# The last norm of a hybrid decoder layer, by two parts of its tokens

## The chip, the cores and the metric

The kernel runs on one core of a Trainium2 chip. The metric is the device time of one launch in microseconds (us); times told of the whole kernel are medians of several runs. A profile is of one execution, and its own time stands beside its span below.

## The reference

One inference step of a one-layer decoder trunk, for a prompt of 256 tokens and 8 samples of 8 tokens, together 320 tokens of width 2048. The layer has two halves; the change lies in the end of the second:

```python
f, new_ffn_conv = conv_ffn(rms_norm(x, p["norm_ffn_pre"]), ffn_conv_state, ...)
x = x + rms_norm(f, p["norm_ffn_post"])

def rms_norm(x, w):
    y = x * lax.rsqrt(jnp.mean(x * x, axis=-1, keepdims=True) + EPS)
    return y * w

def conv_ffn(h, conv_state, w_up, conv_w, conv_b, w_down):
    up = h @ w_up
    up, new_conv = causal_depthwise_conv(up, conv_state, conv_w, conv_b)
    g, u = jnp.split(up, 2, axis=-1)
    return (jax.nn.gelu(g, approximate=True) * u) @ w_down, new_conv
```

The inner width is 5632. The norm at the end needs, for each token, the mean square over all 2048 outputs of the last product, so it can begin for a token only when every block of outputs of that token is there. The output y is x after this line; call x before it x1.

## The kernel before, in words

**Layout.** Features lie on the 128 partitions, tokens along the free axis: an activation of width 2048 is 16 blocks of 128 partitions x 320 tokens. Every product keeps the weights as the stationary operand (128 x 128) and streams the 320 tokens.

**Products.** Each f32 operand is split into two fp32r parts, hi and lo, and a product is three: hi x hi, hi x lo, lo x hi (`accumulate`, lines 127 to 131: line 129 weight hi with x hi, 130 weight hi with x lo, 131 weight lo with x hi). Each of the three loads its weights. `slab` (110 to 125) brings 128 x 1024 weights: a 512 KB DMA on SyncE's queue (115) into `wraw`, hi by a cast on ScalarE (118), lo by a subtraction on VectorE (120). All three tiles have 3 buffers.

**The feed-forward half.** The 5632 inner columns are taken in 11 chunks of 512. `ffn_up` (1061) makes a chunk's inner activations `fhi` and `flo`, 4 blocks of 128 x 320; it reads `h_hi` and `h_lo`, the split input of 16 blocks each. `chunk_out` (205) multiplies the chunk into the 16 output blocks: for each block 4 k-steps of three products into one PSUM bank (the pool `mm` has 4 banks, the pool `ms` 4 more), then VectorE adds the bank to `acc_ffn` in SBUF (217). One `slab` covers a pair of output blocks. The loop (1145 to 1152) makes chunk g + 1's activations before it multiplies chunk g out, so nothing but `chunk_out` is left for the last chunk.

**The last chunk.** Behind each block, `last` (1139) squares the block (ScalarE, lines 281 and 300) and adds the square to the sum `sq4`: on GpSimd (282) for blocks 1 to 12, on VectorE (302) for 13 and 14; block 15's square stays apart (`one`). Then ScalarE scales the block by the norm's weight (1142).

**The tail.** `token_sums` (258) adds over the partitions by products with a column of ones, for `sq4` and then for block 15's square; a product with f32 operands is two instructions in the trace. `rsqrt_by_root` (243) makes 1/sqrt from them, in six small operations on VectorE and one on ScalarE; `spread` (267) transposes the result so that it lies on all partitions, twice: one bank (`r4`) for VectorE, a second one that ScalarE copies to SBUF (`r4s`, 273) for GpSimd. Meanwhile `hand_over` (1159) multiplies blocks of x1 with the identity on TensorE, so that VectorE reads them from PSUM (`x1p`). VectorE makes y for blocks 0 to 10, two at a time (1186 the product with r, 1188 the addition of x1), GpSimd blocks 11 to 15 (1193, 1194); SyncE's queue sends VectorE's blocks (1189), ScalarE's queue GpSimd's (1195).

**Order.** The program is written against a scheduler which orders each engine's instructions by priority and by estimated readiness, gives out buffers and sets all semaphores. `tc.high_priority` (as `first()`) pulls instructions ahead; `tc.issue_after(x)` keeps instructions behind x. Each engine runs its own list in order.

Of the kernel before, what the change touches and what calls it, by code (L numbers as in the profile page):

```python
# [9 lines left out]
F32 = mybir.dt.float32  # L10
# [24 lines left out]
def hybrid_step(  # L35
# [68 lines left out]
    def first():  # L104

        return tc.high_priority(offset=200000)

    slab_load = []

    def slab(src, begins=False):  # L110
        n = src.shape[2]
        with tc.high_priority(offset=100000):
            m = n * src.shape[1]
            raw = wp.tile([P, 1024], F32, tag="wraw", name="wraw", bufs=3)
            slab_load.append(sp.dma_start(raw[:, :m].rearrange("p (a n) -> p a n", n=n), src).ins)
            hi = wp.tile([P, 1024], F32R, tag="whi", name="whi", bufs=3)
            for o in (slice(0, P), slice(P, m)) if begins else (slice(0, m),):
                act.copy(hi[:, o], raw[:, o])  # L118
            lo = wp.tile([P, 1024], F32R, tag="wlo", name="wlo", bufs=3)
            dve.tensor_tensor(out=lo[:, :m], in0=raw[:, :m], in1=hi[:, :m].bitcast(F32), op=ALU.subtract)  # L120

        def block(k, c):
            o = k * n + c * P
            return hi[:, o:o + P], lo[:, o:o + P]
        return block

    def accumulate(ps, w, xhi, xlo, first, last):
        whi, wlo = w
        pe.matmul(ps, whi, xhi, start=first, stop=False)  # L129
        pe.matmul(ps, whi, xlo, start=False, stop=False)  # L130
        return pe.matmul(ps, wlo, xhi, start=False, stop=last).ins  # L131
# [70 lines left out]
    acc = None  # L202
    pd_last = []

    def chunk_out(w, ck, hi, lo, begins, done=None, rate=1):

        for nb in range(KD):
            if nb % 2 == 0:
                wb = slab(rows_of(w, 4 * ck, 4, P * nb, 256))
            ps = mm.tile([P, 512], F32, tag="mm", name=f"pd_{ck}_{nb}")  # L210
            for k in range(4):
                made = accumulate(ps[:, :NT], wb(k, nb % 2), hi[:, k, :], lo[:, k, :], k == 0, k == 3)
            with first():
                if begins:
                    act.copy(acc[:, nb, :], ps[:, :NT])
                else:
                    dve.tensor_tensor(out=acc[:, nb, :], in0=acc[:, nb, :], in1=ps[:, :NT], op=ALU.add)  # L217
# [20 lines left out]
        rsqrt_ins.append(ins)  # L238
        return r

    rsqrt_ins, sums_ins = [], []

    def rsqrt_by_root(rest, ps, scale, rows=P):

        v = tp.tile([P, 3], F32, tag="rs_v3", name="rs_v")[:rows]
        r = tp.tile([P, 3], F32, tag="rs_r3", name="rs_r", bufs=3)[:rows]
        t = tp.tile([P, 3], F32, tag="rs_t3", name="rs_t")[:rows]
        s = tp.tile([P, 3], F32, tag="rs_s3", name="rs_s")[:rows]
        dve.tensor_scalar(out=v, in0=rest, scalar1=scale, scalar2=EPS, op0=ALU.mult, op1=ALU.add)
        dve.scalar_tensor_tensor(out=v, in0=ps, scalar=scale, in1=v, op0=ALU.mult, op1=ALU.add)  # L250
        act.activation(s, v, AF.Sqrt)
# [6 lines left out]
    def token_sums(*sqs):  # L258

        ps = misc("tsum")  # L260
        for c, o in enumerate((0, P, NT - P)):
            for i, sq in enumerate(sqs):
                ins = pe.matmul(ps[:, c:c + 1], sq[:, o:o + P], ones[:, 0:1], start=i == 0, stop=i == len(sqs) - 1).ins  # L263
        sums_ins.append(ins)
        return ps[:, 0:3]

    def spread(r, out=None):

        ps = misc("spread")
        for c, o in ((2, NT - P), (0, 0), (1, P)):  # L270
            pe.transpose(ps[:, o:o + P], r[:, c:c + 1].to_broadcast([P, P]), ident)
        if out is not None:
            act.copy(out, ps[:, :NT])
        return ps[:, :NT]

    def add_square(total, x, begins, adder=pool, place=("sq", 2)):
        if begins:
            act.activation(total, x, AF.Square)
        else:
            sq = tp.tile([P, NT], F32, tag=place[0], name="sq", bufs=place[1])  # L280
            act.activation(sq, x, AF.Square)
            adder.tensor_tensor(out=total, in0=total, in1=sq, op=ALU.add)

    def squares_of(total):

        one, held = [], []

        def step(nb):
            if nb < KD - 3:
                add_square(total, acc[:, nb, :], nb == 0)  # L290
                if nb == 0:

                    act.activation(tp.tile([P, 1], F32, name="root_there", bufs=1), total[:, 0:1], AF.Sqrt)
                return
            with first():
                if nb < KD - 1:
                    held.append(misc("sq_ps")[:, :NT])
                else:
                    one.append(tp.tile([P, NT], F32, tag="sq", name="sq", bufs=2))
                act.activation((one or held)[-1], acc[:, nb, :], AF.Square)  # L300
                if nb > KD - 3:
                    dve.tensor_tensor(out=total, in0=total, in1=held.pop(0), op=ALU.add)
        return step, one


    dacs_d = dr.tile([NH, NT + NS], F32, name="dacs_d")
# [748 lines left out]
    with tc.tile_pool(name="fp", bufs=1) as fp:  # L1055
# [80 lines left out]

        squares, one = squares_of(sq4)

        def last(nb):
            a = acc[:, nb, :]  # L1140
            squares(nb)
            act.activation(a, a, AF.Copy, scale=col(prm_at["norm"][2] + nb))

        NG = NF // 4
# [12 lines left out]
        x1p = {}  # L1157

        def hand_over(where, *blocks):
            for nb in blocks:  # L1160
                x1p[nb] = where[0].tile([P, 512], F32, tag=where[1], name="x1p")[:, :NT]
                made = pe.matmul(x1p[nb], ident, x1[:, nb, :], start=True, stop=True)
            return made.ins
        banks, more = (mm, "mm"), (ms, "ms")
        with tc.issue_after(pd_last[-1]):
            most = token_sums(sq4)
        with tc.issue_after(sums_ins[-1]):
            made = hand_over(banks, 0)
        with tc.issue_after(made):
            ps = token_sums(*one)  # L1170
        r = rsqrt_by_root(most, ps, 1.0 / D)
        with tc.issue_after(sums_ins[-1]):
            made = hand_over(banks, 1, 2)
        with tc.issue_after(made):
            r4 = spread(r)
            r4s = fp.tile([P, NT], F32, name="r4s")
            spread(r, r4s)
        hand_over(banks, 3)
        hand_over(more, 4, 5)
        hand_over(banks, 6, 7, 8, 9, 10)  # L1180
        made = None
        for ks in [slice(k, k + 2) for k in range(0, 10, 2)] + [slice(10, 11)]:
            f = acc[:, ks, :]
            n = ks.stop - ks.start
            with tc.issue_after(made) if made else nullcontext():
                dve.tensor_tensor(out=f, in0=f, in1=r4.unsqueeze(1).to_broadcast([P, n, NT]), op=ALU.mult)
            for k in range(n):
                made = dve.tensor_tensor(out=f[:, k, :], in0=f[:, k, :], in1=x1p[ks.start + k], op=ALU.add).ins
            sp.dma_start(o_y[:, ks, :], f)
        for ks in (slice(11, 12), slice(12, 14), slice(14, 16)):  # L1190
            f = acc[:, ks, :]
            n = ks.stop - ks.start
            pool.tensor_tensor(out=f, in0=f, in1=r4s.unsqueeze(1).to_broadcast([P, n, NT]), op=ALU.mult)
            pool.tensor_tensor(out=f, in0=f, in1=x1[:, ks, :], op=ALU.add)
            act.dma_start(o_y[:, ks, :], f)


_OUTS = [
# [81 lines left out]
```

## Time and profile before

| what | us |
|---|---|
| median of 3 runs | 1798.79 (1796.71 to 1799.12) |
| the profiled execution's own time | 1800.87 |
| its span, first to last instruction | 1799.2 |
| TensorE busy | 1776.3 (99%) |
| VectorE, ScalarE, GpSimd busy | 1190.1, 795.4, 295.4 |

A profile row gives an operation's line, engine, operands and shapes. PE is TensorE's products, PEld its weight loads, which overlap them; DVE is VectorE, ACT ScalarE, POOL GpSimd, SP SyncE. In a timeline row the first two numbers are start and length in us; "x6" is six instructions merged, and the bracket names the idle time before the row and what ended it. In a grouped row the numbers behind the bar are the busy time in us and the mean of one in ns, and behind the second bar the idle time before. The profile prints fp32r operands as f32.

### The profile page before, as it was taken

Reading aid. Unit: us, or ns where it says so; the run is one execution under the profiler, and the core shown is the slowest. Engines: PE = TensorE matmul, PEld = TensorE weight load, DVE = VectorE, ACT = ScalarE, POOL = GpSimd, SP = SyncE. Lnnn points to the kernel's source line nnn. Section 1 sums busy time; section 2 is a strip of 40 time slices with the busy share of each in tenths; the row PEclk is TensorE's granted clock in tenths of the full one; section 3 lists DMA queues with packets and bytes.
Section 4 is the critical chain, followed back from the end, with each engine's and each line's share of the span. In section 5 each row is a group of like instructions: output and inputs, shape, how many; then the busy total and the mean of one; then the engine's idle time right before and its main releaser. Section 6 shows DMA issues by size and latency. Waiting matters only on the chain.

```text
span 1799.2 us, 31167 instructions
## 1 busy us (share of the span) xinstructions
PE 1776.3 (99%) x12200; PEld 1741.7 (97%) x12200; DVE 1190.1 (66%) x2048; ACT 795.4 (44%) x1105; POOL 295.4 (16%) x619
## 2 busy tenths in 40 slices
PE   9999999999999999999999999999999999999998
PEld 8999999999889899999999999999999999999997
DVE  5458664556987969776875474747566565656575
ACT  6444454334545446445554433333434343433335
POOL 3102200000431313104331010111101020101004
PEclk9999999999999999999999999999999999999999
DMA  8646544455566574654554555455545554454542
GB/s 276 194 141 195 159 143 152 153 153 177 180 193 192 167 234 147 178 169 146 174 149 151 155 152 151 148 154 153 153 145 154 152 156 145 153 152 153 151 150 102
DMA packets 222226, 292.56 MB, mean 163 GB/s; under 512 B 16672, under 2 KB 150656, under 8 KB 221888
## 3 DMA queue, kind: packets, MB, share of 16 engines
q1 hardware_dynamic: 209392, 268.12, 49.3%
q10 hardware_dynamic: 10304, 14.82, 2.3%
q0 software_dynamic: 2384, 7.64, 1.4%
q8 instruction: 96, 1.57, 0.4%
q14 instruction: 50, 0.41, 0.1%
HBM read 275.71 MB, written 14.82 MB: 161 GB/s over the span
## 4 chain that ended last, share of the span: by engine, by line
PE 92%; DVE 4%; DMA 2%; issue 1%; ACT 1%; POOL 0%; ACTq 0%; DVEq 0%; POOLq 0%
PE ps L129 20%; PE ps L131 19%; PE ps L130 19%; PE pd L129 10%; PE pd L131 10%; PE pd L130 10%; DMA wraw<-in_w_in 1%; DVE wlo L120 1%; PE y_ps L910 1%; PE yo_ps L817 0%; PE up_ps L833 0%; PE sg L670 0%; ACT whi L118 0%; PE tsum L263 0%; PE vt_ps L582 0%
## 5 line engine op out<-in xcount | busy, mean ns | idle before, releaser
L120 DVE TENSOR_TENSOR wlo<-wraw,whi 128x1024 fp32r<-128x1024 f32 (+1 forms) x474 | 587.6, 1240 | 440.0 <-ACT whi L118 438.2
L118 ACT CAST whi<-wraw 128x1024 fp32r<-128x1024 f32 (+1 forms) x475 | 494.7, 1042 | 717.1 <-PE ps L130 414.8
L129 PE MATMUL ps<-h_hi,whi 128*128 128x320 f32 x2524 | 783.5, 311 | 4.0 <-ACT h_hi L346 2.1
L131 PE MATMUL ps<-h_hi,wlo 128*128 128x320 f32 x2524 | 781.4, 310 | 2.1 <-DVE wlo L120 1.9
L130 PE MATMUL ps<-h_lo,whi 128*128 128x320 f32 x2524 | 780.8, 309 | 0.0
L129 PEld LDWEIGHTS ps<-h_hi,whi 128*128 128x128 f32 x2524 | 475.6, 189 | 7.9 <-issue 2.7
L131 PEld LDWEIGHTS ps<-h_hi,wlo 128*128 128x128 f32 x2524 | 475.4, 188 | 4.1 <-DVE wlo L120 3.5
L130 PEld LDWEIGHTS ps<-h_lo,whi 128*128 128x128 f32 x2524 | 475.6, 188 | 0.7 <-DVE h_lo L546 0.2
L129 PE MATMUL pd<-fhi,whi 128*128 128x320 f32 x704 | 217.2, 309 | 0.0
L131 PE MATMUL pd<-fhi,wlo 128*128 128x320 f32 x704 | 217.2, 309 | 0.0
L130 PE MATMUL pd<-flo,whi 128*128 128x320 f32 x704 | 217.2, 308 | 0.0
L129 PE MATMUL pd<-ohi,whi 128*128 128x320 f32 x448 | 139.6, 312 | 0.0
L131 PE MATMUL pd<-ohi,wlo 128*128 128x320 f32 x448 | 138.4, 309 | 0.0
L130 PE MATMUL pd<-olo,whi 128*128 128x320 f32 x448 | 138.3, 309 | 0.0
L130 PEld LDWEIGHTS pd<-flo,whi 128*128 128x128 f32 x704 | 132.2, 188 | 0.0
L129 PEld LDWEIGHTS pd<-fhi,whi 128*128 128x128 f32 x704 | 132.2, 188 | 0.0
L131 PEld LDWEIGHTS pd<-fhi,wlo 128*128 128x128 f32 x704 | 132.2, 188 | 0.0
L1091 POOL COPY ptf<-pad 128x2 f32<-128x2 f32 x88 | 21.0, 238 | 621.1 <-DVE pad L1079 620.4
L217 DVE TENSOR_TENSOR acc_ffn<-acc_ffn,pd 128x320 f32<-128x320 f32 x160 | 77.6, 485 | 37.9 <-PE pd L131 36.4
L129 PEld LDWEIGHTS pd<-ohi,whi 128*128 128x128 f32 x448 | 84.1, 188 | 1.4 <-issue 0.6
L131 PEld LDWEIGHTS pd<-ohi,wlo 128*128 128x128 f32 x448 | 84.1, 188 | 0.5 <-issue 0.4
L130 PEld LDWEIGHTS pd<-olo,whi 128*128 128x128 f32 x448 | 84.2, 188 | 0.2
(301 smaller groups left out, 1592.3 us busy)
## 6 DMA issues: line engine op xcount, KB each, us to landing
wraw<-in_ffn_w_up SPq DMA_DIRECT2D x176, 512.0 KB, 3.7
wraw<-in_w_in SPq DMA_DIRECT2D x144, 512.0 KB, 3.7
wraw<-in_ffn_w_down SPq DMA_DIRECT2D x88, 512.0 KB, 3.5
wraw<-in_w_out SPq DMA_DIRECT2D x64, 512.0 KB, 3.5
st<-in_state_ssm SPq DMA_DIRECT2D x32, 256.0 KB, 4.5
out_ssm_state_sample<-st ACTq DMA_DIRECT2D x30, 256.0 KB, 4.6
cs<-dacs_d SPq DMA_DIRECT2D x16, 320.0 KB, 4.3
xr<-in_xT SPq DMA_DIRECT2D x4, 640.0 KB, 4.0
```

The costliest lines, as they stand in the source:

```text
L118: act.copy(hi[:, o], raw[:, o])
L120: dve.tensor_tensor(out=lo[:, :m], in0=raw[:, :m], in1=hi[:, :m].bitcast(F32), op=ALU.subtract)
L129: pe.matmul(ps, whi, xhi, start=first, stop=False)
L130: pe.matmul(ps, whi, xlo, start=False, stop=False)
L131: return pe.matmul(ps, wlo, xhi, start=False, stop=last).ins
L217: dve.tensor_tensor(out=acc[:, nb, :], in0=acc[:, nb, :], in1=ps[:, :NT], op=ALU.add)
L910: pe.matmul(ps[64 * i:64 * i + 64, cols], w(hl), x(hl, m, cpx), tile_position=(0, 64 * i), **flags)
L1091: pool.tensor_copy(ptf[:, k, :], pad[:, 256:258])
```

## The change

The last chunk's output blocks 0 to 3 are multiplied as before, for all 320 tokens. Blocks 4 to 15 are multiplied twice: first for tokens 128 to 319 (192 columns), then for tokens 0 to 127 (128 columns). Their weights are loaded from memory and split once: the hi and lo of the pairs at blocks 4 to 12 go to five parts of the memory of `h_hi` and `h_lo`, which no product reads any more, and the pair at 14 to the usual buffers. Sums of squares, root and transposes run once for each part. Those of the first part stand between the second part's products: the sums ahead of its third block, the transposes ahead of its sixth. The transposes of both parts go to one PSUM bank, which VectorE reads and which ScalarE copies for GpSimd.

y of the first part is made beside the second part's products: blocks 0 to 9 on VectorE, which now reads x1 from SBUF, blocks 10 to 15 on GpSimd, all sent on SyncE's queue. y of the second part comes at the end: blocks 0 to 10 on VectorE in groups of 4, 4 and 3, with x1 handed over by TensorE, blocks 11 to 15 on GpSimd in groups of 2 and 3.

The diff, cut to its core (`token_sums`, `spread` and `rsqrt_by_root` take the columns to work on; `squares_of` takes the part's tokens):

```diff
-    def slab(src, begins=False):
+    def slab(src, begins=False, keep=None):
...
-            hi = wp.tile([P, 1024], F32R, tag="whi", name="whi", bufs=3)
+            hi = keep[0] if keep else wp.tile([P, 1024], F32R, tag="whi", name="whi", bufs=3)
...
-            lo = wp.tile([P, 1024], F32R, tag="wlo", name="wlo", bufs=3)
+            lo = keep[1] if keep else wp.tile([P, 1024], F32R, tag="wlo", name="wlo", bufs=3)
...
+    def block_out(wb, nb, hi, lo, ts, begins, made=None):
+        ps = mm.tile([P, 512], F32, tag="mm", name=f"pd_{nb}")
+        for k in range(4):
+            ins = accumulate(ps[:, ts], wb(k, nb % 2), hi[:, k, ts], lo[:, k, ts], k == 0, k == 3)
...
+                dve.tensor_tensor(out=acc[:, nb, ts], in0=acc[:, nb, ts], in1=ps[:, ts], op=ALU.add)
...
+    PARTS = (slice(P, NT), FROM[1:]), (slice(0, P), FROM[:1])
+
+    def chunk_out_in_parts(w, ck, hi, lo, cut, kept, done, root, at):
+        pairs, step = {}, root(0)
+        for i, (ts, _) in enumerate(PARTS):
+            made = None
+            for nb in range(cut, KD):
+                if i and nb - cut in at:
+                    with tc.issue_after(last):
+                        made = next(step)
+                if not i and nb % 2 == 0:
+                    pairs[nb] = pair_of(w, ck, nb, kept.pop(0) if kept else None)
+                with tc.issue_after(made) if made else nullcontext():
+                    last = block_out(pairs[nb - nb % 2], nb, hi, lo, ts, False)
+                done(nb, ts, KD - 1 - nb)
...
+    def root_in_parts(total, one, out):
+        def root(i):
+            of = PARTS[i][1]
+            with first():
+                most = token_sums(total, of=of)
+                ps = token_sums(one[i], of=of)
+                r = rsqrt_by_root(most, ps, 1.0 / D)
+                yield sums_ins[-1]
+                spread(r, of=of, ps=out)
+                yield spread_ins[-1]
+        return root
...
-            chunk_out(ffn_w_down, g, hi, lo, g == 0, last if g == NG - 1 else None)
+            if g < NG - 1:
+                chunk_out(ffn_w_down, g, hi, lo, g == 0)
+        kept = [[h.rearrange("p k n -> p (k n)")[:, 1024 * i:1024 * i + 1024] for h in hT] for i in range(5)]
+        r4 = misc("spread")
+        root = root_in_parts(sq4, one, r4)
+        chunk_out(ffn_w_down, NG - 1, hi, lo, False, last, blocks=range(4))
+        chunk_out_in_parts(ffn_w_down, NG - 1, hi, lo, 4, kept, last, root, (2, 5))
...
+        ts = PARTS[0][0]
+        with first():
+            act.copy(r4s[:, ts], r4[:, ts])
+        made = None
+        for k in range(0, 10, 2):
+            with tc.issue_after(made) if made else nullcontext():
+                times_r(dve, r4, k, 2, ts)
+                made = plus_x1(dve, x1[:, k:k + 2, ts], k, 2, ts)
+            out(sp, k, 2, ts)
+        for k, behind in (10, sq_added[-4]), (12, sq_added[-1]), (14, sq_added[-1]):
+            with tc.issue_after(behind):
+                times_r(pool, r4s, k, 2, ts)
+                plus_x1(pool, x1[:, k:k + 2, ts], k, 2, ts)
+            out(sp, k, 2, ts)
+        ts = PARTS[1][0]
+        step = root(1)
...
+        for k in range(1, 12):
+            with tc.issue_after(ins):
+                if k in (3, 8):
+                    ins = next(step)
+            with tc.issue_after(ins):
+                ins = hand_over(k)
+        with first():
+            act.copy(r4s[:, ts], r4[:, ts])
+        for k, n in ((0, 4), (4, 4), (8, 3)):
+            with tc.issue_after(made):
+                times_r(dve, r4, k, n, ts)
+                made = plus_x1(dve, x1p[k // 4][:, :n], k, n, ts)
+            out(sp, k, n, ts)
+        for k, n in ((11, 2), (13, 3)):
+            times_r(pool, r4s, k, n, ts)
+            plus_x1(pool, x1[:, k:k + n, ts], k, n, ts)
+            out(act, k, n, ts)
```

More of the change, by code (lines that the diff above doesn't have):

```diff
@@ L203, in hybrid_step, with pair_of, chunk_out @@
     pd_last = []
-    def chunk_out(w, ck, hi, lo, begins, done=None, rate=1):
-        for nb in range(KD):
-            if nb % 2 == 0:
[L209 to L217, printed above, removed]
+    ALL = slice(0, NT)
+    def pair_of(w, ck, nb, keep=None):
+        return slab(rows_of(w, 4 * ck, 4, P * nb, 256), keep=keep)
+    def block_out(wb, nb, hi, lo, ts, begins, made=None):
+        ps = mm.tile([P, 512], F32, tag="mm", name=f"pd_{nb}")
+        for k in range(4):
+            ins = accumulate(ps[:, ts], wb(k, nb % 2), hi[:, k, ts], lo[:, k, ts], k == 0, k == 3)
+            if made is not None:
+                made.append(ins)
+        with first():
+            if begins:
+                act.copy(acc[:, nb, ts], ps[:, ts])
+            else:
+                dve.tensor_tensor(out=acc[:, nb, ts], in0=acc[:, nb, ts], in1=ps[:, ts], op=ALU.add)
+        return ins
+    def chunk_out(w, ck, hi, lo, begins, done=None, rate=1, blocks=range(KD)):
+        for nb in blocks:
+            if nb % 2 == 0:
+                wb = pair_of(w, ck, nb)
+            made = block_out(wb, nb, hi, lo, ALL, begins)
             if done is not None:
@@ L239, in rsqrt_of, with rsqrt_by_root @@
         return r
[L241 to L248, printed above, removed]
+    rsqrt_ins, sums_ins, spread_ins = [], [], []
+    def rsqrt_by_root(rest, ps, scale):
+        n = ps.shape[1]
+        v, r, t, s = (tp.tile([P, 3], F32, tag=f"rs_{i}3", name=f"rs_{i}", bufs=3 if i == "r" else 2)[:, :n] for i in "vrts")
         dve.tensor_scalar(out=v, in0=rest, scalar1=scale, scalar2=EPS, op0=ALU.mult, op1=ALU.add)
@@ L264, in token_sums, with spread @@
         sums_ins.append(ins)
[L265 to L271, printed above, removed]
+        return ps[:, 0:len(of)]
+    def spread(r, out=None, of=FROM, ps=None):
+        if ps is None:
+            ps = misc("spread")
+        for c in sorted(range(len(of)), key=lambda c: -(of[c] % P)):
+            spread_ins.append(pe.transpose(ps[:, of[c]:of[c] + P], r[:, c:c + 1].to_broadcast([P, P]), ident).ins)
         if out is not None:
@@ L1137, in hybrid_step, with last @@
         squares, one = squares_of(sq4)
-        def last(nb):
-            a = acc[:, nb, :]
-            squares(nb)
+        def last(nb, ts=ALL, left=None):
+            a = acc[:, nb, ts]
+            squares(nb, ts, left)
             act.activation(a, a, AF.Copy, scale=col(prm_at["norm"][2] + nb))
@@ L1151, in hybrid_step @@
                 acc = fp.tile([P, KD, NT], F32, name="acc_ffn")
-            chunk_out(ffn_w_down, g, hi, lo, g == 0, last if g == NG - 1 else None)
-        act.dma_start(o_fconv_p, ptf)
[L1157 to L1177, printed above, removed]
@@ new lines, in hybrid_step, with times_r, plus_x1, out @@
+        r4s = fp.tile([P, NT], F32, name="r4s")
+        act.dma_start(o_fconv_p, ptf)
+        def times_r(by, r, k, n, ts):
+            f = acc[:, k:k + n, ts]
+            return by.tensor_tensor(out=f, in0=f, in1=r[:, ts].unsqueeze(1).to_broadcast([P, n, ts.stop - ts.start]), op=ALU.mult).ins
+        def plus_x1(by, x, k, n, ts):
+            f = acc[:, k:k + n, ts]
+            return by.tensor_tensor(out=f, in0=f, in1=x, op=ALU.add).ins
+        def out(by, k, n, ts):
+            by.dma_start(o_y[:, k:k + n, ts], acc[:, k:k + n, ts])
@@ new lines, in hybrid_step, with hand_over @@
+        for k, behind in (10, sq_added[-4]), (12, sq_added[-1]), (14, sq_added[-1]):
[4 more added lines that the diff above has]
+        ts = PARTS[1][0]
+        x1p, ident_at = [], None
+        step = root(1)
+        def hand_over(k):
+            if k % 4 == 0:
+                x1p.append(mm.tile([P, 512], F32, tag="mm", name="x1p").rearrange("p (k n) -> p k n", k=4))
+            return pe.matmul(x1p[-1][:, k % 4], ident, x1[:, k, ts], start=True, stop=True).ins
@@ new lines, in hybrid_step @@
+        ins = hand_over(0)
+        for k in range(1, 12):
[4 more added lines that the diff above has]
+                ins = hand_over(k)
+        with first():
+            act.copy(r4s[:, ts], r4[:, ts])
[4 more added lines that the diff above has]
+            out(sp, k, n, ts)
```

44 lines of the change are left out of this document (16 added, 28 removed).

## The prediction, as put on record

> **What bounds the kernel now.** I read the first lines of the page first, then the chain of work that ended last, then the busy time by stretch around the change, then the timeline of the last 45 us.
>
> ```profile
> span 1799.2 us, 31167 instructions
> ...
> PE 1776.3 (99%) x12200; PEld 1741.7 (97%) x12200; DVE 1190.1 (66%) x2048; ACT 795.4 (44%) x1105; POOL 295.4 (16%) x619
> ...
> PE 92%; DVE 4%; DMA 2%; issue 1%; ACT 1%; POOL 0%; ACTq 0%; DVEq 0%; POOLq 0%
> ```
>
> TensorE (PE) is busy all the span, its weight loads (PEld) almost as long, and 92% of the chain that ended last (the last row) is its work. Whatever makes TensorE's stream of products longer is paid in full; the only stretch not bound by it is the end. The changed kernel's instruction order is the same as before on all five engines up to the preparation of the last chunk's weights, and on TensorE up to block 4 of that chunk, so two stretches matter: the twelve blocks 4 to 15 of the last chunk, and what follows their last product.
>
> ```profile
> 1760.53 0.31 PE L129 MATMUL pd<-fhi,whi 128*128 128x320 f32 x1
> ...
> 1781.50 0.31 PE L131 MATMUL pd<-fhi,wlo 128*128 128x320 f32 x1
> 1781.65 0.81 PE L263 MATMUL tsum<-ones,sq 128*128 128x1 f32 x6
> ```
> ```profile
> 1760.53:1781.65 21.12, 21.12 (x146) 21.04 (x145) 11.79 (x19) 16.27 (x30) 12.34 (x12) 1.00 0.16 51
> 1781.65:1799.20 17.55, 9.51 (x42) 5.70 (x40) 10.53 (x24) 1.66 (x4) 7.71 (x6) 0.81 0.39 149
> ```
>
> The columns are length, then busy time of PE, PEld, DVE, ACT and POOL, granted clock, DMA share and GB/s. Twelve blocks of 12 products are 144; from 1760.53 to the next instruction behind them at 1781.65 they take 21.12 us, 146.7 ns each, at full clock with no gap. The other 17.55 us are the tail: the norm's root, y, its transfers. The change makes the first stretch into 288 narrower products and shortens the second.
>
> **TensorE: 288 products for 144.** Each block is multiplied twice, for 192 tokens and later for 128. The columns that stream through the array are the same in all (144 x 320), but each product loads its 128 x 128 weights, so the loads double. What a load costs when the product behind it is too short to cover it:
>
> ```profile
> L131 PEld LDWEIGHTS pd<-fhi,wlo 128*128 128x128 f32 x704 | 132.2, 188 | 0.0
> L426 PEld LDWEIGHTS ps_dt<-h_hi,whi_dt 128*64 128x64 f32 x16 | 2.1, 134 | 0.2
> L263 PEld LDWEIGHTS tsum<-ones,sq 128*128 128x128 f32 x30 | 3.8, 191 | 1.0 <-ACT sq L300 0.8
> ```
> ```profile
> 1781.63 0.74 PEld L263 LDWEIGHTS tsum<-ones,sq 128*128 128x128 f32 x6
> ```
>
> The token sums stream one column behind each load of 128. Six loads take 0.74 us and one takes 191 ns, so they start (740 - 191) / 5 = 110 ns apart: nothing but the load sets that pace. Those operands are f32, the products' are fp32r, but a load of the products takes the same 188 ns; and between the fp32r loads of 64 and of 128 columns lie 54 ns, so 128 columns are 108 ns and the other 80 ns are latency that overlaps the load before. By streaming, 192 columns are 146.7 x 192/320 = 88 ns and 128 columns 59 ns, both under 110. So I take **110 ns** for each of the 288 products (ends: 107 and 115 ns): 31.68 us in place of 21.12, **+10.56 us**.
>
> [...]
>
> The first part's norm goes between the second part's products: two columns of sums from two tiles, 4 instructions, 8 records (an f32 product is two passes: the row above has 6 records for 3 instructions), and two transposes: 10 x 0.11 = **+1.10 us**. Both stand late enough: the sums come two blocks (2.6 us) behind the first part's last product, and before, 1.30 us lay between the last product and the sum of its squares; the transposes come three blocks (4.0 us) behind the sums, against 2.4 us in the rows that follow. The products therefore end at 1760.53 + 31.68 + 1.10 = 1793.31 instead of 1781.65: 11.66 us later.
>
> **The tail.** Its steps before:
>
> ```profile
> 1781.85 0.49 DVE L217 TENSOR_TENSOR acc_ffn<-acc_ffn,pd 128x320 f32<-128x320 f32 x1 [0.27 <-PE pd L131]
> ...
> 1782.43 0.47 ACT L300 ACTIVATE sq<-acc_ffn 128x320 f32<-128x320 f32 x1 [0.78 <-DVE acc_ffn L217]
> ...
> 1782.95 0.83 PE L263 MATMUL tsum<-ones,sq 128*128 128x1 f32 x6
> ...
> 1783.82 0.16 DVE L250 SCALAR_TENSOR_TENSOR rs_v<-tsum,rs_v 128x3 f32<-128x3 f32 x1 [1.16 <-PE tsum L263]
> ...
> 1785.34 0.82 PE L271 MATMUL spread<-ident,rs_r 128*128 128x128 f32 x6
> 1785.87 0.82 DVE L1186 TENSOR_TENSOR acc_ffn<-acc_ffn,spread 128x640 f32<-128x640 f32 x1 [0.85 <-PE spread L271]
> ...
> 1786.20 0.42 ACT L273 COPY r4s<-spread 128x320 f32<-128x320 f32 x1 [1.98 <-PE spread L271]
> 1786.70 2.36 POOL L1193 TENSOR_TENSOR acc_ffn<-acc_ffn,r4s 128x320 f32<-128x320 f32 x2 [8.05 <-ACT r4s L273]
> 1786.73 0.89 DVE L1188 TENSOR_TENSOR acc_ffn<-acc_ffn,x1p 128x320 f32<-128x320 f32 x2
> ...
> 1794.93 0.49 DVE L1188 TENSOR_TENSOR acc_ffn<-acc_ffn,x1p 128x320 f32<-128x320 f32 x1
> ```
> ```profile
> L1186 DVE TENSOR_TENSOR acc_ffn<-acc_ffn,spread 128x640 f32<-128x640 f32 x5 | 4.1, 817 | 0.9 <-PE spread L271 0.9
> L1193 POOL TENSOR_TENSOR acc_ffn<-acc_ffn,r4s 128x640 f32<-128x640 f32 x2 | 3.1, 1540 | 0.0
> L1193 POOL TENSOR_TENSOR acc_ffn<-acc_ffn,r4s 128x320 f32<-128x320 f32 x1 | 0.9, 860 | 8.1 <-ACT r4s L273 8.1
> L1186 DVE TENSOR_TENSOR acc_ffn<-acc_ffn,spread 128x320 f32<-128x320 f32 x1 | 0.5, 482 | 0.0
> ```
>
> VectorE's 817 and 482 ns give 1.05 ns an element and 0.15 us fixed; GpSimd's 1540 and 860 give 2.1 ns and 0.18 us. ScalarE's square of 320 is 0.47 us and its root of 3 elements 0.20:
>
> ```profile
> L251 ACT ACTIVATE rs_s<-rs_v 128x3 f32<-128x3 f32 x1 | 0.2, 204 | 0.5 <-DVE rs_v L250 0.5
> L1142 ACT ACTIVATE acc_ffn<-acc_ffn,prm 128x320 f32<-128x320 f32 x16 | 9.0, 562 | 0.4
> out_y<-acc_ffn SPq DMA_DIRECT2D x1, 160.0 KB, 2.5
> ```
>
> so its square of 128 is 0.31. Counted from the end of the products, for 128 tokens:
> - add from 0.20 to 0.49 (0.29 for 0.49), square from 0.58 to 0.89, sum at 0.94;
> - two records instead of six, so the root's second step comes 0.87 - 4 x 0.11 = 0.43 later, 1.37; from there to the transposes 1.52 as before: 2.89;
> - one transpose instead of six, then ScalarE's copy: 0.86 - 5 x 0.11 = 0.31 later, 3.20, for 0.28. Before, VectorE read a bank of its own and waited for TensorE alone; now both read one bank, and VectorE's multiplication waits for that copy: 3.56 for both engines;
> - VectorE: groups of 4, 4 and 3 blocks, a multiplication and an addition each: 512 elements 0.68 us, 384 elements 0.55, with 0.03 between: 1.42 + 1.42 + 1.14, end at 7.54. GpSimd: 256, 384, 256, 384 elements: 0.72 + 1.0 + 0.72 + 1.0, end at 7.0, ahead of VectorE;
> - from VectorE's last end (1795.42) to the span's end 3.78 us, taken as it is, as the last transfer (the third row above; 192 KB for 160) is of the same kind.
>
> So 11.32 us in place of 17.55: **-6.23 us**.
>
> **What I cost at nothing.** The first part's y on VectorE, ten operations of 384 elements, 5.5 us, and its share on GpSimd, six of 1.0 us, lie beside the second part's products (15.8 us). GpSimd's last two groups wait for the squares of block 12, which are summed 3 x 1.32 - 1.1 (add, square, sum) = 2.9 us ahead of the products' end, and take 4.0 us: done 1.1 us behind it, 2.4 us before r is there for the second part. Beside VectorE's long operations GpSimd is slower, in the second row here, which the first overlaps, than in the third, alone:
>
> ```profile
> 1765.90 1.23 DVE L120 TENSOR_TENSOR wlo<-wraw,whi 128x1024 fp32r<-128x1024 f32 x1 [1.16 <-ACT whi L118]
> 1766.38 1.48 POOL L282 TENSOR_TENSOR sq<-sq,sq 128x320 f32<-128x320 f32 x1 [1.01 <-ACT sq L281]
> 1768.23 0.88 POOL L282 TENSOR_TENSOR sq<-sq,sq 128x320 f32<-128x320 f32 x1 [0.37 <-ACT sq L281]
> ```
>
> At 1.48/0.88 on all of it the 4.0 us would become 6.7 and miss the cover by 0.3 us. Per block ScalarE needs 0.36 us for the square and 0.42 for the scaling (562 ns at 320) and VectorE 0.35, against 12 x 0.11 = 1.32: they keep up. The weights: pairs 4 to 12 now go to the memory of the finished h and wait no longer for a buffer that TensorE must release; in the changed kernel's order VectorE prepares those of block 12 ahead of the sum of block 3, so they are there early. If they weren't, pairs at the old pace of 3.52 us instead of 2.64 would cost 5 x 0.88 = 4.4 us. The first part's y transfers are queued on SP behind the last weight load, so nothing that TensorE needs waits for them.
>
> **The sum.** 10.56 + 1.10 - 6.23 = **+5.4 us**. On the profiled execution's own 1800.87 us (span 1799.2 and 1.7 around it) that is 1806.3; its time is 2.1 over the median of the three runs, 1798.79, and on that I predict **1804.2 us**. With loads of 107 to 115 ns (-0.9 to +1.4) and the tail's gain between 5 and 7, the forecast's own range is +2.6 to +8: 1801.4 to 1807.
>
> **Rivals.** (1) *The doubled loads stay hidden*, and narrow products take 88 and 59 ns by their columns: the 21.12 us remain, and 1.10 - 6.23 = -5.1 gives 1793.7, faster. The point from which it decides is a mean product of (21.12 + 6.23 - 1.10) / 288 = 91 ns. For it: the loads of now overlap by 41 ns (188 long, 147 apart). Against: the sums' loads, with nothing to cover, still come 110 apart. Chance 0.05. A milder form, half hidden, midway between 110 and these at 85 and 99 ns: 144 x 0.184 = 26.5 us, +0.3, 1799.1, no measurable change; 0.03. [...]
>
> (2) *The second part waits.* VectorE's queue is in order: the root of the first part and ten y operations stand between the sums of blocks 5 and 11. If r or ScalarE's copy comes late, the block sums behind them wait, and TensorE has only four banks, three blocks or 4.0 us of cover against 5.5 us of y; or weights come late (4.4 us), or GpSimd is late. Price +2 to +4.4 more: some 1808. For it: GpSimd's 1.48 us row. Against: three block sums stand among those ten operations. Chance 0.14.
>
> (3) *A narrow fp32r product runs as an f32 one*, in two passes. The trace has no fp32r product narrower than 320 columns, and each is one record (704 of a form above are 11 chunks of 16 blocks of 4); f32 ones take two, six for three blocks of x1:
>
> ```profile
> 1783.64 1.86 PE L1162 MATMUL x1p<-acc_mix,ident 128*128 128x320 f32 x6
> ```
>
> (1.86 - 0.48) / 5 = 0.277 us a record at 320 columns, so 0.166 and 0.111: 144 x 2 x 0.277 = 79.8 us, +53.5 in all, 1852. Nothing in the trace speaks for it but that no narrow one is in it. Chance 0.06.
>
> **How the numbers follow.** Forecast 0.72, rivals 0.08, 0.14 and 0.06. A change under 0.2% (3.6 us) is about what a measurement here can't tell from none; 0.08 of the forecast's chance lies under it. So faster 0.05, same 0.08 + 0.03 = 0.11, slower 0.84. The range takes the forecast's bounds and most of rival 2: 1800.8 to 1809.5; outside lie rivals 1 and 3 and the ends.
>
> **What would show it.** The narrow products' starts: 110 ns apart in both parts says right; 88 and 59 says rival 1; two records a product, rival 3. The stretch from block 4's first product to the second part's last should be 32.8 us, with no idle of TensorE in it that names VectorE, ScalarE or GpSimd; idle there is rival 2. From the last product to the end should be 11.3 us, with VectorE's last group at the end of it. I am wrong if a product costs under 91 ns.

## The result, and the profile after

| | before | changed |
|---|---|---|
| median, us (6 runs each) | 1798.95 (1796.71 to 1805.07) | 1817.98 (1814.54 to 1822.31) |
| ratio, 95% interval | | 1.0103 [1.0088, 1.0119] |
| profiled execution, us (span) | 1800.87 (1799.2) | 1822.31 (1820.3) |

Slower, as forecast, but by 19 us where 5.4 were forecast, outside the range.

The windows of the changed kernel's TensorE work, cut where the products change; columns as in the prediction, the granted clock being the third from the end:

```profile
1762.38:1778.44 16.06, 16.06 (x146) 16.06 (x145) 8.28 (x19) 14.11 (x33) 8.79 (x12) 1.00 0.02 7
1778.44:1782.43 3.99, 3.99 (x38) 3.99 (x37) 1.25 (x5) 2.33 (x8) 0.83 (x2) 1.00 0.00 0
1782.43:1807.50 25.07, 25.07 (x121) 25.07 (x120) 9.71 (x25) 6.66 (x20) 9.26 (x14) 0.50 0.19 63
1807.50:1820.30 12.80, 6.16 (x30) 5.97 (x30) 4.93 (x13) 1.18 (x4) 3.32 (x4) 0.63 0.28 82
```

The first row is the part of 192 tokens: 144 products in 16.06 us, 111.5 ns each where 110 were forecast. The second and third are the part of 128 tokens: 29.06 us where 16.94 were forecast. TensorE is busy in all of it and waits for nobody; the clock is 1.00 for 4 us and **0.50** for the other 25. The timeline shows the moment:

```profile
1781.09 1.00 PE L278 MATMUL tsum<-ones,sq 128*128 128x1 f32 x8
...
1782.32 0.29 PE L130 MATMUL pd<-fhi,h_hi 128*128 128x128 f32 x1
1782.43 0.39 PE L131 MATMUL pd<-flo,h_hi 128*128 128x128 f32 x1
1782.62 0.42 PE L132 MATMUL pd<-fhi,h_lo 128*128 128x128 f32 x1
1782.84 0.42 PE L130 MATMUL pd<-fhi,h_hi 128*128 128x128 f32 x1
```

From 1782.43 on the starts are 213 ns apart instead of 111. It is the loads that have slowed: they set the pace of narrow products (111.5 ns at 192 and at 128 columns alike), and they follow the clock. Their row in the second part, behind the fall, and in the first part (minimum, median and maximum in ns):

```profile
L130 PEld LDWEIGHTS pd<-fhi,h_hi x30: 333/333/338, 1782.7 to 1801.6; 128*128 128x128 f32 x30
...
L130 PEld LDWEIGHTS pd<-fhi,h_hi x39: 192/192/192, 1762.6 to 1775.3; 128*128 128x128 f32 x39
```

The profiles' start of block 4 lies anywhere from 1756.07 to 1764.37 us in the runs told here, though no edit but one touches what is ahead of it; so stages below are counted from that start. Before: 21.12 us of products and 17.55 of tail, 38.67. Changed: 45.12 (16.06 + 29.06) and 12.80, 57.92. The difference is 19.25 us, the measured one 19.0. Against the forecast, the products are 12.3 us too long and the tail 1.5.

Why did the clock fall there? The first batch of experiments was to tell two theories apart; both fell, and a third came out of them.

### The profile page after: what moved, and what is told of

Its sections match the earlier page's. It is cut to its first block, busy times and chain, and to the rows that moved or that the text cites. A ratio compares the mean times of both kernels' runs of the same rounds, so it can differ in the third digit from the quotient of the medians.

```text
span 1820.3 us, 31539 instructions
## 1 busy us (share of the span) xinstructions
PE 1799.2 (99%) x12343; PEld 1767.7 (97%) x12343; DVE 1192.7 (66%) x2067; ACT 801.2 (44%) x1131; POOL 296.8 (16%) x632
## 4 chain that ended last, share of the span: by engine, by line
PE 89%; DVE 6%; DMA 2%; issue 1%; ACT 1%; POOL 1%; ACTq 0%; DVEq 0%; POOLq 0%
PE ps L130 19%; PE ps L132 18%; PE ps L131 18%; PE pd L130 10%; PE pd L132 10%; PE pd L131 10%; DVE wlo L121 2%; DMA wraw<-in_w_in 1%; DVE cv L441 1%; PE y_ps L963 1%; ACT whi L119 0%; PE yo_ps L870 0%; PE up_ps L886 0%; DVE acc_mix L223 0%; PE sg L723 0%
## 5 line engine op out<-in xcount | busy, mean ns | idle before, releaser
L121 DVE TENSOR_TENSOR wlo<-wraw,whi 128x1024 fp32r<-128x1024 f32 (+1 forms) x469 | 581.4, 1240 | 435.3 <-ACT whi L119 433.4
L119 ACT CAST whi<-wraw 128x1024 fp32r<-128x1024 f32 (+1 forms) x470 | 489.4, 1042 | 712.8 <-PE ps L131 413.6
L130 PE MATMUL pd<-fhi,whi 128*128 128x320 f32 (+2 forms) x672 | 207.8, 309 | 0.0
L131 PE MATMUL pd<-flo,whi 128*128 128x320 f32 (+2 forms) x672 | 207.8, 309 | 0.0
L132 PE MATMUL pd<-fhi,wlo 128*128 128x320 f32 (+2 forms) x672 | 207.8, 309 | 0.0
L130 PEld LDWEIGHTS pd<-fhi,whi 128*128 128x128 f32 x672 | 127.4, 190 | 0.0
L131 PEld LDWEIGHTS pd<-flo,whi 128*128 128x128 f32 x672 | 127.4, 190 | 0.0
L132 PEld LDWEIGHTS pd<-fhi,wlo 128*128 128x128 f32 x672 | 127.4, 190 | 0.0
L223 DVE TENSOR_TENSOR acc_ffn<-acc_ffn,pd 128x320 f32<-128x320 f32 (+2 forms) x172 | 79.1, 462 | 51.3 <-PE pd L132 50.0
```

The source lines that it names most:

```text
L223: dve.tensor_tensor(out=acc[:, nb, ts], in0=acc[:, nb, ts], in1=ps[:, ts], op=ALU.add)
```

## The experiments

Each differs from the changed kernel by the edit shown, unless another is named. "Stage" is from the first narrow product to the span's end in the profile, products + tail; before has 38.67 and the changed kernel 57.92. Ratios are to the kernel before, on the same chip.

### 1. The second part streams 192 columns, 128 of them used

```diff
-            ins = accumulate(ps[:, ts], wb(k, nb % 2), hi[:, k, ts], lo[:, k, ts], k == 0, k == 3)
+            tw = slice(0, 192) if ts == slice(0, P) else ts
+            ins = accumulate(ps[:, tw], wb(k, nb % 2), hi[:, k, tw], lo[:, k, tw], k == 0, k == 3)
```

> The second part's products stream 192 columns (tokens 0 to 191) and only the 128 of tokens 0 to 127 are used; loads, instructions and order are those of the changed kernel. Theory A (TensorE's clock halves because 128 columns behind a load of 110 ns keep the array streaming under half of the time): the clock stays at 1.0 in both parts, products stay 111 ns apart, the second part takes about 17 us instead of 29, and the time is 4 to 7 us above the kernel before. Theory B (the clock halves because the sums and transposes of one or a few columns stand between the products): the clock still falls 1 us behind those sums, 18 to 20 us above before.

Measured: 1811.13 us, ratio 1.0050 [1.0034, 1.0065]; stage 33.79 + 12.50 = 46.29 us. The windows of the second part and the tail:

```profile
1779.06:1796.80 17.74, 17.42 (x157) 17.25 (x155) 10.22 (x29) 7.97 (x25) 6.81 (x12) 1.00 0.20 67
1796.80:1809.30 12.50, 3.94 (x31) 3.40 (x29) 5.94 (x15) 1.87 (x6) 6.61 (x8) 0.86 0.39 117
```

More columns and less time: the clock holds, 17.74 us for 29.06. So the sums alone don't lose the clock (theory B falls), and width matters. By the ratio that is +9.0 us, over the 4 to 7 that theory A gave: TensorE waits 0.32 us in it for one of VectorE's block sums, and the tail is 1.2 us over the forecast's.

### 2. The first part's sums and transposes late

```diff
-        chunk_out_in_parts(ffn_w_down, NG - 1, hi, lo, 4, kept, last, root, (2, 5))
+        chunk_out_in_parts(ffn_w_down, NG - 1, hi, lo, 4, kept, last, root, (10, 11))
```

> The first part's sums move from ahead of the second part's third block to ahead of its eleventh, the transposes to ahead of its twelfth. Theory A: the clock still falls to half about 4 us into the second part (1782 to 1783 on the trace's scale), with nothing but products there; time 18 to 23 us above before, the y of the first part now being late. Theory B: the clock stays at 1.0 until the sums, about 13 us into the second part; time 7 to 11 us above before.

Measured: 1812.55 us, ratio 1.0068 [1.0053, 1.0084]; stage 33.39 + 16.16 = 49.55, the tail long because y of the first part now comes late. The second part:

```profile
1777.30:1794.64 17.34, 17.30 (x156) 17.19 (x155) 5.25 (x21) 9.09 (x27) 4.35 (x10) 1.00 0.00 1
```

128-column products keep the full clock for over 13 us when nothing stands between them. So width alone doesn't lose it either (theory A falls). By the ratio the time is +12.2 us, a little over theory B's 7 to 11.

The row holds more than that. Its last 4 us are the same mixture as in the changed kernel, with the sums here:

```profile
1790.68 1.00 PE L278 MATMUL tsum<-ones,sq 128*128 128x1 f32 x8
```

Yet the clock stays at 1.00 to the end of the products and falls only at 1797.67, in the tail. The last section comes back to this.

### 3. The parts change places

```diff
-    PARTS = (slice(P, NT), FROM[1:]), (slice(0, P), FROM[:1])
+    PARTS = (slice(0, P), FROM[:1]), (slice(P, NT), FROM[1:])
```

with the hand-over of x1 two blocks to a bank, the second part's transposes two hand-overs earlier, and VectorE's last groups 2, 2, 2, 2, 2 and 1.

> The two parts change places: tokens 0 to 127 first, then tokens 128 to 319 (the tail then has 192 tokens, groups of 2 blocks, transposes ahead of the seventh hand-over). Theory A: the clock falls to half 3 to 5 us into the first part, which then takes about 27 us, and rises again 3 to 7 us into the second part although the sums and transposes stand there; time 17 to 24 us above before. Theory B: the first part runs at 1.0 with 111 ns a product (16 us), the clock falls in the second part behind the sums.

Measured: 1809.30 us, ratio 1.0050 [1.0031, 1.0069]; stage 32.66 + 15.32 = 47.98. The first part (128 columns) and the second (192, with the sums):

```profile
1759.72:1775.74 16.02, 16.02 (x146) 16.02 (x145) 7.56 (x19) 13.15 (x33) 7.53 (x12) 1.00 0.01 4
1775.74:1792.38 16.64, 16.64 (x151) 16.64 (x151) 8.67 (x29) 8.85 (x24) 7.36 (x12) 1.00 0.16 48
```

The kinds of work of the changed kernel, paired the other way, and no fall anywhere. A first part of 128 tokens needs one column of sums and not two, so there are four one-column loads here for eight, and this run is the weaker for it. But experiments 1 and 2 already say that it takes both: 128-column products **and** the sums among them. Theory C, formed here: the clock follows the share of time in which columns stream, over a window of some 3 to 4 us.

The shares told below are estimates, from the 320-column products' 146.7 / 320 = 0.458 ns a column and 111.5 ns a product: 53% at 128 columns, 59% at 144, 66% at 160 and 79% at 192. Eight one-column loads take 0.86 us out of some 3.4, which leaves 39, 44, 49 and 59%. The expectations count less for a column, which no run here shows; their shares are a tenth lower, in the same order, and theory A's "under half" at 128 columns is 53% by the rows.

### 4. The doubled products alone

The kernel before, each block split in place:

```diff
-            for k in range(4):
-                made = accumulate(ps[:, :NT], wb(k, nb % 2), hi[:, k, :], lo[:, k, :], k == 0, k == 3)
+            for ts in (slice(P, NT), slice(0, P)) if done is not None and nb > 3 else (slice(0, NT),):
+                for k in range(4):
+                    made = accumulate(ps[:, ts], wb(k, nb % 2), hi[:, k, ts], lo[:, k, ts], k == 0, k == 3)
```

> The kernel before with one edit: blocks 4 to 15 of the last chunk multiply 128 to 319 and then 0 to 127 block by block, 288 products for 144, everything behind them as before. Theory A and my term of the sum: products 111 ns apart whichever width, columns streaming 60% of the time over each block, clock at 1.0, +10.9 us (10 to 12) over before. If the clock falls even here the limit lies above 60% and the time is 20 us or more above before. If narrow products cost less than I took, it is under +9.

The condition holds in the layer's first half too, whose last chunk ends with a norm as well, so 24 blocks were split and not 12; the expectation is for 12. Measured: 1821.70 us, ratio 1.0119 [1.0103, 1.0135], +20.6, so 10.3 for each twelve. The last chunk's blocks 4 to 15 and the tail:

```profile
1775.29:1807.40 32.11, 32.11 (x291) 32.11 (x289) 12.11 (x19) 16.81 (x30) 12.66 (x12) 1.00 0.10 34
1807.40:1824.90 17.50, 9.08 (x42) 5.65 (x41) 10.53 (x24) 1.66 (x4) 7.73 (x6) 0.87 0.39 150
```

32.11 / 288 = 111.5 ns a product: +11.0 us where the forecast had +10.56, with the tail as before (17.50 to 17.55).

### 5. The first part's sums stream 128 columns

```diff
+        n = P if of == FROM[1:] else 1
...
-                ins = pe.matmul(ps[:, c:c + 1], sq[:, o:o + P], ones[:, 0:1], start=i == 0, stop=i == len(sqs) - 1).ins
+                ins = pe.matmul(ps[:, n * c:n * c + n], sq[:, o:o + P], ones[:, 0:n], start=i == 0, stop=i == len(sqs) - 1).ins
...
-        return ps[:, 0:len(of)]
+        return ps[:, 0:n * len(of):n]
```

> The changed kernel with one edit: the first part's token sums stream 128 columns of ones instead of one (the same eight instructions' worth of loads at the same place; the first of equal columns is used). Theory C (the clock follows the share of time in which columns stream, taken over some 3 to 4 us: 128-column products alone give 48% and keep it, eight one-column loads among them bring it to about 36% and lose it): the clock stays at 1.0 through the second part, which takes 17 us, and the time is 6 to 10 us above before, as with 192 columns. Theory B' (any f32 products of a norm between 128-column products lose it, however wide): the clock falls as in the changed kernel, 18 to 20 us above before.

Measured: 1805.85 us, ratio **1.0030** [1.0016, 1.0043]; stage 33.37 + 12.16 = 45.53. The sums, then the second part:

```profile
1774.96 1.10 PE L279 MATMUL tsum<-ones,sq 128*128 128x128 f32 x8
```
```profile
1772.31:1789.44 17.13, 17.13 (x157) 17.13 (x155) 10.09 (x29) 8.11 (x25) 6.64 (x12) 1.00 0.20 67
```

The same eight loads at the same place, the next product 0.86 us behind their start as in the changed kernel; only the columns that stream behind them differ, 128 for 1. The clock holds and the second part takes 17.13 us instead of 29.06. Theory C holds, B' falls. The time is a little under what I expected.

### 6. 192 columns, and the sums three times over

Experiment 1, and:

```diff
-        for c, o in enumerate(of):
+        for c, o in list(enumerate(of)) * (3 if of == FROM[1:] else 1):
```

> The kernel whose second part streams 192 columns, with the first part's sums taken three times over: 24 one-column loads, 2.7 us, instead of 8. Theory C: the share over the window falls to about 20 to 30% even beside 192-column products, so the clock falls to half behind the sums; then 192 columns behind a half-speed load stream 75% of the time, and it rises again 3 to 7 us later: about +1.8 us for the loads and +3 to +6 us for the half clock against the kernel with the sums once. Theory B': width decides, no fall, +1.8 us alone.

Measured: 1813.02 us, ratio 1.0063 [1.0032, 1.0095]; stage 36.65 + 13.16 = 49.81, 3.5 us over experiment 1. The stretches around the sums (1778.13 to 1780.75), and the stretch that follows:

```profile
1775.50:1780.00 4.50, 4.50 (x44) 4.50 (x42) 1.09 (x4) 2.28 (x7) 0.92 (x2) 1.00 0.00 0
1780.00:1786.00 6.00, 6.00 (x40) 6.00 (x41) 1.39 (x7) 1.21 (x4) 0.45 (x1) 0.72 0.01 3
1786.00:1792.00 6.00, 6.00 (x56) 6.00 (x56) 4.96 (x11) 2.03 (x7) 1.18 (x3) 1.00 0.28 91
```

Enough one-column loads lose the clock even beside 192 columns, and those win it back: a mean of 0.72 over 6 us at 0.5 and 1.0 is 3.4 us at half clock, the expected dip. The share had fallen to (3.4 - 2.6) / 3.4 x 79% = 19%, a little under the 20 to 30 I gave. The price was less than I expected: 3.5 us by the stages, where 1.8 and another 3 to 6 were to come.

### 7. Spare one-column products among 128-column ones

Experiment 2, and four products that nothing reads, ahead of the second part's third block:

```diff
+                if i and nb - cut == 2:
+                    with tc.issue_after(last):
+                        with first():
+                            spare = misc("spare")
+                            for c in range(4):
+                                made = pe.matmul(spare[:, c:c + 1], ident, ones[:, 0:1], start=True, stop=True).ins
```

> The kernel with the first part's root late (whose clock held for 13 us of 128-column products), with four spare f32 products of one column, eight loads, ahead of the second part's third block, where the changed kernel has its sums; nothing reads them and they wait for nothing but the block before. Theory C: the clock falls to half within 4 us of them, and the time is 12 to 18 us above before-with-late-root's own +11 to +12, as the second part's remaining blocks run at half clock. If waiting for the norm's own work is what loses the clock, it stays at 1.0 up to the real sums and the time is 1 us above that kernel's.

Measured: 1822.62 us, ratio 1.0118 [1.0084, 1.0153]; stage 44.89 + 14.94 = 59.83, 10.3 over experiment 2. The spare products stand at 1781.98; the second part up to 4 us in, and the rest of it:

```profile
1779.33:1783.32 3.99, 3.99 (x39) 3.99 (x37) 0.93 (x3) 2.31 (x7) 0.83 (x2) 1.00 0.00 0
1783.32:1808.16 24.84, 24.84 (x128) 24.84 (x128) 5.40 (x20) 6.75 (x20) 4.61 (x10) 0.54 0.00 1
```

The clock falls behind them as in the changed kernel. It isn't the norm, nor a wait for it. I had expected 12 to 18 us over experiment 2: the longer second part gave 11.5 and took 1.2 off the tail.

### 8. Two parts of 160

```diff
-    PARTS = (slice(P, NT), FROM[1:]), (slice(0, P), FROM[:1])
+    PARTS = (slice(160, NT), (160, 192)), (slice(0, 160), (0, 32))
```

with x1 handed over three blocks to a bank and VectorE's last groups 3, 3, 3 and 2.

> The two parts have 160 tokens each (tokens 160 to 319 first; sums over windows of 128 that overlap; x1 handed over three blocks to a bank). Theory C: products stream 60% of 111 ns, with the sums 44% over the window; if the limit lies under that the clock holds in both parts, the products' stretch is 33 to 34 us and the time 6 to 10 us above before; if the clock falls, the limit lies between 44 and 53% (192 columns with sums held) for a window with sums and the 48% of plain 128-column products contradicts it.

Measured: 1806.05 us, ratio 1.0030 [1.0014, 1.0045]; stage 33.20 + 12.76 = 45.96. The second part:

```profile
1780.20:1797.34 17.14, 17.14 (x156) 17.14 (x155) 9.18 (x29) 8.50 (x24) 6.95 (x12) 1.00 0.20 56
```

The clock holds: 66% alone and 49% with the sums suffice. By the ratio the time is +5.4 us, a little under the 6 to 10 I expected.

### 9. Six blocks by parts

Experiment 5, and:

```diff
-        chunk_out(ffn_w_down, NG - 1, hi, lo, False, last, blocks=range(4))
-        chunk_out_in_parts(ffn_w_down, NG - 1, hi, lo, 4, kept, last, root, (2, 5))
+        chunk_out(ffn_w_down, NG - 1, hi, lo, False, last, blocks=range(10))
+        chunk_out_in_parts(ffn_w_down, NG - 1, hi, lo, 10, kept, last, root, (2, 4))
```

> The kernel with wide sums, but only blocks 10 to 15 are multiplied by parts (144 narrow products for 72; the transposes come two blocks behind the sums). By the term of the sum, narrow products at 111 ns with the clock at 1.0: 16.0 + 1.1 us for 10.6, so +6.5 in place of +11.7, against the same tail of -6.2, less up to 3 us where VectorE's y of the first part (5.5 us in a second part of 9 us) delays the last blocks: 0 to +3 us against before. If the cost is not the doubled loads but something paid once, it stays at +5 or more.

Measured: 1806.14 us, ratio 1.0022 [1.0006, 1.0037]. Both parts and the tail:

```profile
1772.49:1780.51 8.02, 8.02 (x75) 8.02 (x73) 2.97 (x8) 5.78 (x14) 4.22 (x6) 1.00 0.01 2
1780.51:1789.60 9.09, 9.09 (x85) 9.09 (x83) 4.12 (x14) 4.14 (x13) 2.72 (x5) 1.00 0.01 2
1789.60:1805.70 16.10, 6.08 (x31) 5.54 (x30) 9.63 (x24) 1.87 (x6) 9.33 (x9) 0.62 0.52 163
```

The products follow the term: 17.11 us where 17.1 were expected, 6.5 over the 10.56 before. But the tail is 16.10 for 12.16: nine microseconds don't cover y of the first part, and VectorE is busy 9.63 us of the tail for 6.12 in experiment 5. Half the doubling, and most of the gain in the tail is gone with it; that is why it is still slower, by the ratio +4.0 us where 0 to +3 were expected.

### 10. The second part streams 144 columns

Experiment 1 with 144 for 192.

> The second part's products stream 144 columns and 128 of them are used; sums of one column in their place as in the changed kernel. Theory C: products alone stream 54%, with the sums 40% over a window; 36% lost the clock and 44% (160 columns) held it, so this lies between and tells on which side the limit is: with the clock held +5 to +10 us over before, with it lost +16 to +20.

Measured: 1807.80 us, ratio 1.0031 [1.0018, 1.0044]; stage 33.97 + 12.06 = 46.03. The second part:

```profile
1780.42:1798.34 17.92, 17.37 (x157) 17.22 (x155) 10.41 (x29) 7.97 (x25) 6.81 (x12) 1.00 0.20 67
```

Held at 59% alone, 44% with the sums. In the profiled execution an edge of the clock's window splits the sums (last section), which makes it 47%; the mean clocks of all six executions, 0.995 and 0.996, show no long fall in any. So the limit that holds the clock lies between 39 and some 44 to 47% by that count.

## Why the prediction was wrong, point by point

**The step that failed:** "So I take 110 ns for each of the 288 products". For the 144 of 192 columns it was right (111.5), and for 288 in place too (experiment 4: +11.0 us where I had +10.56). For the second part it was right only until the clock fell: in the last 25.07 us the products came 213 ns apart. I read the pace of a load from rows at full clock and never asked what would keep the clock there; "what would show it" says 110 in both parts. No rival had it. The price is 29.06 for 16.94 us, **12.1** of the 13.8 us by which the stages miss the forecast.

**The cause:** products of 128 columns stream about half of the time, since each waits for its load; the first part's sums, eight loads with one column behind each, bring the share over some 3.4 us to about 39%, and the clock halves. Three edits show it: with the loads and their order kept, more columns in the products (1, 10) or more columns in the sums (5) keep the clock; and eight one-column loads that nothing reads lose it where it was held without them (7). This isn't the luck of the profiled executions: the mean clock over a whole execution was 0.987 to 0.990 in all six of the changed kernel, 0.986 and 0.987 in both of experiment 7, and 0.994 to 0.997 in all twelve of experiment 5, whose second part has products as narrow. Why the clock doesn't come back is argued: at half clock the loads come 213 ns apart, so if a column takes twice as long too, the share is still some 55%. The trace had a hint of it all: in the tail before, TensorE's clock was 0.81 on the mean.

The rows say one thing more: at half clock the profile has TensorE busy for 25.07 of 25.07 us, so what counts isn't whether instructions run.

**What was right:** the direction; the pace of loads at full clock; the first part's norm among the products (the first part's 16.06 and 1.1 us); nothing of rivals 1 and 3. With the clock kept (experiment 5) the same plan costs 1.0030 [1.0016, 1.0043], and the forecast's +5.4 us on 1798.79 is 1.0030; that they agree to the last digit is luck, as the stages of the profile give +6.9 (45.53 for 38.67). The cover of y by the second part held too, with TensorE at no time waiting for it, but in the changed kernel that was luck: the second part had become 12 us longer. With the clock kept TensorE waited for one of VectorE's block sums 0.32 us in experiment 1 and 0.55 in experiment 10, and not at all in experiment 5: rival 2, in small.

**A slip in the working.** The forecast's own range, +2.6 to +8, doesn't follow from its ends: 107 ns and a gain of 7 give 9.7 + 1.1 - 7 = +3.8. It touches only the lower end of the range, and the measured time lies above the upper one. No run shows the 107 ns either: the sums' loads start 110 ns apart before and 111 in the changed kernel ((0.97 - 0.19) / 7, from the row of its eight at 1781.03), and the narrow products 111.5.

**The tail** was forecast at 11.32 us and took 12.80, of which the half clock is part: the hand-overs ahead of the sums end 1.38 us (1807.50 to 1808.88) behind the products' end, and the transpose starts 0.93 us behind r (1810.94 to 1811.87; 0.05 in experiment 5). With the clock kept it is 12.16. There rival 2's late GpSimd shows in small. VectorE's and GpSimd's rows at experiment 5's tail:

```profile
1788.62 0.46 POOL L301 TENSOR_TENSOR sq<-sq,sq 128x128 f32<-128x128 f32 x1 [0.18 <-ACT sq L300]
...
1789.04 1.96 POOL L1221 TENSOR_TENSOR acc_ffn<-acc_ffn,r4s 128x384 f32<-128x384 f32 x2
...
1790.95 1.96 POOL L1225 TENSOR_TENSOR acc_ffn<-acc_ffn,acc_mix 128x384 f32<-128x384 f32 x2
...
1792.01 0.92 DVE L265 SCALAR_TENSOR_TENSOR rs_t<-rs_v,rs_r 128x1 f32<-128x1 f32 x1
1792.96 0.16 DVE L266 TENSOR_TENSOR rs_t<-rs_t,rs_r 128x1 f32<-128x1 f32 x1
```

GpSimd ends the first part's y 3.5 us behind the products (1792.91 to 1789.44) and not 1.1. Its last two groups take 3.9 us, as priced (4.0), but they begin 0.4 us ahead of the products' end and not 2.9: the square of block 12, for which they wait, is summed only by 1789.08 (the first row). VectorE's block sums had stood behind the first part's y in its list; those of blocks 11 to 13 run together from 1787.16. Beside GpSimd's last operation, an operation of one element a partition takes 0.92 us (0.16 in the changed kernel, at 1810.39, with GpSimd idle) and ends when GpSimd does (1792.93 and 1792.91): 0.76 of the 0.84 us. That GpSimd held it up is argued from the rows; no experiment was made on it.

## What to carry to other kernels

Splitting a product's columns doubles its weight loads, and below some 240 columns (an estimate: 110 ns at 0.458 ns a column) the load is what is paid; price it from a row where one column streams. Then ask what share of the time columns stream: narrow products that keep TensorE busy all the time can still cost the clock, and a few one-column products among them can halve it for what follows (here eight records, and 0.50 for 25.07 us). Where such sums must stand there, let them stream more columns than they need; behind a load that is paid anyway this cost nothing here (0.86 us for the eight, with one column or 128).

## What the runs showed of the hardware that I had not expected

- TensorE's clock halved while it was busy: at 128 columns a load, with eight one-column loads among the products, 0.50 for 25 us; at 128 columns without them, or 144 to 192 with them, 1.00. Loads slowed with it, from 192 to 333 ns long and from 111 to 213 ns apart.
- It came back within 3.4 us beside products of 192 columns (experiment 6; some 83% at half clock, by the same estimate) and not in 25 us beside products of 128 (some 55%). So what holds the clock and what wins it back differ, by this count; where the second limit lies stays open, and so does whether columns are what is counted or something that goes with them.
- The changes of the granted clock keep to a step in time, whatever the work: they lie whole multiples of 3.41 us apart. Before, the clock is at 0.50 from 242.96 to 246.37, from 847.12 to 853.94 and from 1792.61 on; the changes after the first come 1, 177, 179 and 454 steps behind it. The changed kernel has it from 1782.45 to 1813.17, nine steps, and experiment 6 from 1781.65 to 1785.06, one. Taking a step as the window, the fall comes at the end of one, 1.4 us behind the first one-column product in the changed kernel and 3.5 in experiments 6 and 7. This fits the late sums of experiment 2: counted back by two windows from the fall at 1797.67, an edge lies at 1790.84, inside the sums, which took 0.16 us from one window and 0.70 from the next (some 42% by the same count). In the profiled executions of experiments 1, 5 and 10 an edge falls into the sums as well, so one profile doesn't show that those edits keep the clock; for experiment 5 the twelve mean clocks do. That an edge inside the sums saved the clock in experiment 2 is argued from its rows.
